# Casts and low parts of the mixer's weights at first rank in the scheduler's order

## The chip, the cores and the metric

The kernel runs on one core of a Trainium2 chip. The metric is the device time of one execution in microseconds. A core has engines that each take their own instructions one after the other and that wait for each other by semaphores: TensorE (PE in the profile, with its weight loads as PEld), VectorE (DVE), ScalarE (ACT), GpSimd (POOL) and SyncE (SP), which here only issues DMAs.

## The reference

One decoder layer on 256 tokens of width 2048 in float32: a feed-forward network, a token mixer, and a second feed-forward network, each with a residual sum and a layer norm behind it.

```python
x = layer_norm(ALPHA * x + 0.5 * swiglu(x, ffn1_w_gate, ffn1_w_up, ffn1_w_down), ln1_g, ln1_b)
(c_q, c_kv, k_rope, q_nsa, k_c, v_c, k_s, v_s, k_w, v_w, g_nsa) = split_cols(x @ w_in, IN_SIZES)
o_mla = mla_attention(c_q, c_kv, k_rope, ...)        # 8 heads, latent ranks 512 and 256, causal softmax
o_nsa = nsa_attention(q_nsa, k_c, v_c, k_s, ...)     # 8 heads: compressed, selected and window branch, gated
mix = jnp.concatenate([o_mla, o_nsa], axis=-1) @ w_out
x = layer_norm(ALPHA * x + mix, ln2_g, ln2_b)
x = layer_norm(ALPHA * x + 0.5 * swiglu(x, ffn2_w_gate, ffn2_w_up, ffn2_w_down), ln3_g, ln3_b)
```

The hidden width of the feed-forward networks is 5632. The mixer's weights are w_in (2048 columns in, 3416 out), two up-projections of the latent attention (uq and ukv), the small matrices of the block compression, and w_out (2048 x 2048).

## The kernel before

**Three products for one.** [...] `split(hi, lo, src)` (L94 to L96) does this: ACT casts the source to the high part (L95), and DVE subtracts the high part from the source, which gives the low part (L96). `mm3` (L98 to L102) then issues three matmuls into one PSUM bank: high by high (L100), high activations by low weights (L101), low activations by high weights (L102). In the names of the profile, `whi` and `wlo` are the parts of a weight piece, `thi` and `tlo` those of transposed activations; `raw` and `sum` are the buffers into which the pieces are loaded.

**Buffers.** A weight piece is 128 x 1024 values (two blocks of 128 rows, 512 columns). Raw pieces come into 5 buffers of the pool `rawp` or 3 of `sump`, by turns. The high parts have 6 buffers (`hip`), the low parts 6 (`lop`). So a cast needs three things: its piece has landed, one of the 6 high buffers has been released by TensorE's last matmul on it, and ACT is free. [...]

**The mixer's weights** all come through `load` (L149). It issues the DMA on SP (L171, or the paired form above it), takes a high and a low buffer, and splits. With `spare` set it splits into tiles of the attention's pool instead and returns earlier (L172 to L178); this is so for the first two pieces of the mixer's first product. `load` is called by `gemm` (input projection, ukv, output projection), `gemm_T` (the up-projections whose result is wanted transposed) and `out_last` (the last columns of w_out). The feed-forward weights do not come this way: `gemm2` splits them itself, in its inner function `parts`.

**Order of the work.** The order of PE and SP is that of the program text (`manual_schedule` for these two engines). The other engines are ordered by the scheduler of the Tile layer when the program is built: it keeps a timeline of its own, and where several instructions of one engine are ready, the one with the best rank goes first. The rank is the place in the program text, unless the instruction stands in a `tc.high_priority()` block, which gives it a rank at the start of the program. At run time each engine keeps the order that came out of this, and waits at an instruction whose inputs or buffers are not ready, with all that stands behind it.

In the kernel before, two things stand in such blocks: the normalisation of a row block in `ln` (from the mean and variance, L598, to the scaling of the rows, L610 and L612), and, with `first` set, the scaling and the split of the first transposed tile behind a layer norm in `norm_T` (L577 to L588).

**Attention beside the projections.** The text interleaves large products with small work by hand. A product counts time in ticks, `tick(n)` advances them, and generators that were given to `spawn` run on between the pieces: each yields a number of ticks and so sets how far behind an evaluation on ACT and DVE the dependent instruction of PE is placed. For a softmax this is DSM = 4 ticks; two ticks are one piece, 12 matmuls of 512 columns. A softmax unit runs through: scores from PSUM with scale and mask on DVE (L804), row maximum on DVE (L777), exponentials on ACT (L781), their sums and reciprocals on DVE (L788, L789, with a gate L791), scaling of the rows on ACT (L794) or DVE (L796), transposes on PE (L812), and the copy of these to SBUF on ACT (L814). The block compression has a chain of small steps on DVE and ACT (L969 to L975, a gelu), matmuls from raw buffers (L956) and a last matmul (L980 or L986). `ln_res` (L622 to L630) multiplies the residual rows by gain and bias on DVE; nothing waits for it before the output projection. `norm_T` transposes rows on PE (L575), scales them on ACT (L583, for even groups of four columns) or DVE (L585), and splits them (L95 and L96 with `thi` and `tlo`).

In the text, a weight piece's split stands directly ahead of its own matmuls. The softmax steps of an earlier tick stand ahead of it.

Of the kernel before, what the change touches and what calls it, by code (L numbers as in the profile page):

```python
# [53 lines left out]
def layer(ctx: ExitStack, tc: tile.TileContext, a: dict, out: bass.AP):  # L54
# [24 lines left out]
    def am2(dt=F32):  # L79

        m = am(dt)
        return m[:, 0:4, :], m[:, 4:8, :]
# [11 lines left out]
    def split(hi, lo, src):  # L94
        A.copy(hi, src)  # L95
        V.tensor_tensor(lo, src, f(hi), op=OP.subtract)  # L96
# [45 lines left out]
    def new_raw():  # L142

        turn[0] += 1
        return (sump if turn[0] % 8 >= 5 else rawp).tile([P, KT, NCH], F32, name="sum" if turn[0] % 8 >= 5 else "raw")
# [3 lines left out]
    def load(w, c, pc, spare=False):  # L149

        if (id(w), c, pc[0]) in ahead:
            return ahead.pop((id(w), c, pc[0]))
        ap, pairs, n = w[:3]
        paired = len(w) > 3
        k0, kn = pc[0], len(pc)
        assert pc == list(range(k0, k0 + kn)) and k0 // KT == pc[-1] // KT
        r0 = (c * pairs + k0 // KT) * P
        raw = new_raw()
        order = list(range(kn))
        if paired:  # L160

            r0 = (c // 2 * pairs + k0 // KT) * P
            src = w[3][r0:r0 + P].rearrange("p (i j n) -> p i j n", i=2, j=2)[:, :, c % 2, :]
            if c % 2:
                order = order[::-1]
            if kn < KT:
                at = k0 % KT if c % 2 == 0 else 1 - k0 % KT
                src = src[:, at:at + 1]
            nc.sync.dma_start(raw[:, :kn, :n], src)
        else:  # L170
            nc.sync.dma_start(raw[:, :kn, :n], ap[r0:r0 + P].rearrange("p (k n) -> p k n", k=KT)[:, k0 % KT:k0 % KT + kn])  # L171
        if spare:  # L172
            out = []
            for j in range(kn):
                hi, lo = (m.rearrange("p a b -> p (a b)")[:, :n] for m in am2(F32R))
                split(hi, lo, raw[:, j, :n])
                out.append((hi, lo))
            return [out[j] for j in order]  # L178
        hi = hip.tile([P, KT, NCH], F32R, name="whi")
        lo = lop.tile([P, KT, NCH], F32R, name="wlo")  # L180
        split(hi[:, :kn, :n], lo[:, :kn, :n], raw[:, :kn, :n])
        return [(hi[:, j, :n], lo[:, j, :n]) for j in order]

    def new_bank():
# [2 lines left out]
    def gemm(x, w, c, ks, finish, head=0, tail=0, spare=0, first=KT, each=None, nxt=None):  # L187
# [20 lines left out]
        for r in ([pcs[:head]] if head else []) + mid + ([pcs[len(pcs) - tail:]] if tail else []):  # L208
            end = r[-1] is pcs[-1]
            held = []  # L210
            for pc in r:
                held.append((pc, load(w, c, pc, at == 0 and len(held) < spare)))
                go(0, *held[-1])
                if len(r) > 1:
                    tick(1)
            if end:
                if nxt:
                    ahead[id(nxt[0]), nxt[1], nxt[2]] = load(nxt[0], nxt[1], [nxt[2] + j for j in range(KT)])
                finish(0, ps[0])
            for h in held:  # L220
                go(1, *h)
                if len(r) > 1:
                    tick(1)
            if end:
                finish(1, ps[1])
            if len(r) == 1:
                tick(2)
            if each:
                each(at)
            at += 1  # L230

    def gemm_T(xs, w, c, ks, finish, nxt):

        wp = {}
        for i in range(0, len(ks), KT):
            wp.update(zip(ks[i:i + KT], load(w, c, ks[i:i + KT])))
        nb = w[2] // P  # L240
        for i in range(nb // 2):
            ps = new_bank().rearrange("p (b s) -> p b s", b=2)
            for j in range(2):
                cs = slice((2 * i + j) * P, (2 * i + j + 1) * P)
                for k in ks:
                    (wh, wl), (xh, xl) = wp[k], xs(k)
                    PE.matmul(ps[:, j], wh[:, cs], xh, start=k == ks[0], stop=False)
                    PE.matmul(ps[:, j], wh[:, cs], xl, start=False, stop=False)
                    PE.matmul(ps[:, j], wl[:, cs], xh, start=False, stop=k == ks[-1])
                tick(1)  # L250
            if i == nb // 2 - 1 and nxt:
                ahead[id(nxt[0]), nxt[1], nxt[2]] = load(nxt[0], nxt[1], [nxt[2] + j for j in range(KT)])
            finish(i, ps)
# [942 lines left out]
```

## Time and profile before

| | us |
|---|---|
| three runs | 1755.46 (median), 1753.73, 1756.78 |
| the profiled execution | 1755.67 |
| its span, first to last instruction | 1754.0 |

The granted clock of TensorE was 0.998 over the span. By the windows of busy time, with the borders rounded to where the stages change, in us:

| stage | length | TensorE | VectorE | ScalarE |
|---|---|---|---|---|
| first feed-forward network, 0 to 690 | 690 | 685.87 | 656.76 | 418.67 |
| its end, the mixer, 690 to 1040 | 350 | 347.47 | 241.70 | 181.30 |
| second layer norm, second network, last layer norm, 1040 to 1754 | 714 | 702.02 | 688.37 | 421.82 |

How to read the rows that follow. A group has line, engine, operation, the tile that is written and those that are read, shapes and count; behind the first bar stand the busy time and the mean in ns of one, behind the second the idle time of the engine just before and what ended it. In the timeline a row has start, duration and the instruction; "x2" is two in a row merged into one, and the bracket names the idle time of that engine before it and what ended it. Ends of matmuls are modelled and overlap the next start, so for TensorE the distance from start to start is what counts. In the DMA rows the last number is the median time from issue to landing.

### The profile page before, as it was taken

Reading aid. Unit: us, or ns where it says so; the run is one execution under the profiler, and the core shown is the slowest. Engines: PE = TensorE matmul, PEld = TensorE weight load, DVE = VectorE, ACT = ScalarE, POOL = GpSimd, SP = SyncE. Lnnn points to the kernel's source line nnn. Section 1 sums busy time; section 2 is a strip of 40 time slices with the busy share of each in tenths; the row PEclk is TensorE's granted clock in tenths of the full one; section 3 lists DMA queues with packets and bytes.
Section 4 is the critical chain, followed back from the end, with each engine's and each line's share of the span. In section 5 each row is a group of like instructions: output and inputs, shape, how many; then the busy total and the mean of one; then the engine's idle time right before and its main releaser. Section 6 shows DMA issues by size and latency. Waiting matters only on the chain. (4 is left out here: it accounts for less than half of the span.)

```text
span 1754.0 us, 22419 instructions
## 1 busy us (share of the span) xinstructions
PE 1735.4 (99%) x8040; PEld 1428.0 (81%) x8040; DVE 1586.8 (90%) x2099; ACT 1021.8 (58%) x1354; POOL 17.0 (1%) x39
## 2 busy tenths in 40 slices
PE   9999999999999999999999999999999999999997
PEld 7888888887888888887788788888888888888886
DVE  7899999999999999865586679899999999999998
ACT  6656565565656656654365555565665565656652
POOL 0000000000000000000000001000000000000000
PEclk9999999999999999999999999999999999999999
DMA  9665656555666457646753355655666555565655
GB/s 334 220 214 167 213 197 214 192 192 190 210 204 229 172 196 245 192 156 214 260 193 120 122 179 170 214 192 172 212 206 211 202 192 199 197 211 193 205 202 181
DMA packets 100336, 350.01 MB, mean 200 GB/s; under 512 B 11136, under 2 KB 13696, under 8 KB 100224
## 3 DMA queue, kind: packets, MB, share of 16 engines
q1 hardware_dynamic: 98944, 344.39, 58.2%
q0 software_dynamic: 1280, 4.20, 0.9%
q8 instruction: 63, 1.03, 0.2%
q14 instruction: 49, 0.40, 0.1%
HBM read 346.44 MB, written 2.10 MB: 199 GB/s over the span
## 5 line engine op out<-in xcount | busy, mean ns | idle before, releaser
L100 PE MATMUL bank<-whi,thi 128*128 128x512 f32 (+1 forms) x1904 | 747.9, 393 | 0.6 <-ACT whi L95 0.6
L101 PE MATMUL bank<-wlo,thi 128*128 128x512 f32 (+1 forms) x1904 | 740.3, 389 | 3.1 <-DVE wlo L96 3.1
L102 PE MATMUL bank<-whi,tlo 128*128 128x512 f32 (+1 forms) x1904 | 739.5, 388 | 0.0
L95 ACT CAST whi<-raw 128x1024 fp32r<-128x1024 f32 (+1 forms) x577 | 539.9, 962 | 265.1 <-PE bank L102 140.1
L96 DVE TENSOR_TENSOR wlo<-raw,whi 128x1024 fp32r<-128x1024 f32 (+1 forms) x577 | 630.9, 1109 | 60.5 <-ACT whi L95 59.2
L95 ACT CAST whi<-sum 128x1024 fp32r<-128x1024 f32 x271 | 282.6, 1049 | 341.6 <-DVE sum L328 137.5
L100 PEld LDWEIGHTS bank<-whi,thi 128*128 128x128 f32 x1904 | 357.7, 188 | 78.1 <-issue 4.1
L101 PEld LDWEIGHTS bank<-wlo,thi 128*128 128x128 f32 x1904 | 357.8, 188 | 77.4 <-DVE wlo L96 6.5
L102 PEld LDWEIGHTS bank<-whi,tlo 128*128 128x128 f32 x1904 | 357.5, 188 | 73.5
L96 DVE TENSOR_TENSOR wlo<-sum,whi 128x1024 fp32r<-128x1024 f32 x271 | 324.7, 1216 | 30.9 <-ACT whi L95 28.9
L101 PE MATMUL bank<-wlo,m 128*128 128x512 f32 x448 | 174.4, 389 | 0.4 <-DVE wlo L96 0.4
L102 PE MATMUL bank<-whi,m 128*128 128x512 f32 x448 | 174.3, 389 | 0.0
L100 PE MATMUL bank<-whi,m 128*128 128x512 f32 x448 | 174.3, 389 | 0.0
L326 DVE TENSOR_TENSOR sum<-raw 128x1024 f32<-128x1024 f32 x112 | 136.6, 1220 | 11.2 <-DMA raw<-in_ffn_w_up 9.0
L101 PEld LDWEIGHTS bank<-wlo,m 128*128 128x128 f32 x448 | 84.1, 188 | 18.5 <-DVE wlo L96 0.9
L102 PEld LDWEIGHTS bank<-whi,m 128*128 128x128 f32 x448 | 84.1, 188 | 17.4
L100 PEld LDWEIGHTS bank<-whi,m 128*128 128x128 f32 x448 | 84.1, 188 | 17.4
L328 DVE TENSOR_TENSOR sum<-sum,raw 128x512 f32<-128x512 f32 x112 | 76.7, 685 | 0.2
L327 DVE TENSOR_TENSOR sum<-sum,raw 128x512 f32<-128x512 f32 x112 | 76.7, 685 | 0.1
L384 DVE TENSOR_TENSOR w<-bank,w 128x512 f32<-128x512 f32 x80 | 51.8, 682 | 1.4 <-PE bank L102 1.4
L781 ACT ACTIVATE w<-w,mx 128x256 f32<-128x256 f32 (+1 forms) x48 | 21.3, 446 | 27.7 <-DVE mx L777 24.7
L516 DVE TENSOR_TENSOR w<-w 128x512 f32<-128x512 f32 x40 | 25.7, 684 | 0.0
(187 smaller groups left out, 938.4 us busy)
## 6 DMA issues: line engine op xcount, KB each, us to landing
raw<-in_ffn_w_down SPq DMA_DIRECT2D x176, 512.0 KB, 4.4
raw<-in_ffn_w_up SPq DMA_DIRECT2D x160, 512.0 KB, 4.8
raw<-in_ffn_w_gate SPq DMA_DIRECT2D x146, 512.0 KB, 4.8
raw<-in_ffn_gu SPq DMA_DIRECT2D x32, 512.0 KB, 4.9
raw<-in_w_in SPq DMA_DIRECT2D x30, 512.0 KB, 5.3
raw<-in_w_out SPq DMA_DIRECT2D x20, 512.0 KB, 3.3
sum<-in_w_in SPq DMA_DIRECT2D x18, 512.0 KB, 5.5
sum<-in_ffn_w_gate SPq DMA_DIRECT2D x12, 512.0 KB, 4.8
```

Source lines behind the costliest of these rows:

```text
L95: A.copy(hi, src)
L96: V.tensor_tensor(lo, src, f(hi), op=OP.subtract)
L100: PE.matmul(ps, xh, wh, start=first and not onto, stop=False, skip_group_check=onto)
L101: PE.matmul(ps, xh, wl, start=False, stop=False, skip_group_check=onto)
L102: PE.matmul(ps, xl, wh, start=False, stop=last, skip_group_check=onto)
L326: V.tensor_tensor(t13, a_, b_[:, 1:2, :].broadcast_to([P, 2, NCH]), op=OP.add)
L327: V.tensor_tensor(t24[:, 0], t13[:, 0], a_[:, 1], op=OP.add)
L328: V.tensor_tensor(t24[:, 1], t24[:, 0], b_[:, 0], op=OP.add)
L384: V.tensor_tensor(r, B[b], rest[b], op=OP.add)
L516: V.tensor_tensor(hs[c0 + j, t], r, sg[c0 + j, t], op=OP.mult)
L781: A.activation(s[:, h, :], s[:, h, :], AF.Exp, bias=mx[:, h:h + 1], accum_out=sm[:, h:h + 1])
```

## The change

The call of `split` for pieces that go to the high and low buffers, in `load`, stands in a `tc.high_priority()` block. Casts and subtractions of the mixer's weights so get a rank at the start of the program; the two spare pieces, the feed-forward weights, and the splits of activations keep theirs. The DMA stays outside the block.

```diff
@@ -178,7 +178,8 @@
             return [out[j] for j in order]
         hi = hip.tile([P, KT, NCH], F32R, name="whi")
         lo = lop.tile([P, KT, NCH], F32R, name="wlo")
-        split(hi[:, :kn, :n], lo[:, :kn, :n], raw[:, :kn, :n])
+        with tc.high_priority():
+            split(hi[:, :kn, :n], lo[:, :kn, :n], raw[:, :kn, :n])
         return [(hi[:, j, :n], lo[:, j, :n]) for j in order]
```

## The prediction

> **What bounds the kernel now.** I read the page's engine shares first, then busy time by window, the groups of the mixer (690 to 1040 us), its waits, and the timeline around each wait.
>
> ```profile
> span 1754.0 us, 22419 instructions
> PE 1735.4 (99%) x8040; PEld 1428.0 (81%) x8040; DVE 1586.8 (90%) x2099; ACT 1021.8 (58%) x1354; POOL 17.0 (1%) x39
> ```
>
> TensorE is busy 99% of the span. The profiled execution took 1755.67 us, 1.67 more than its span and 0.2 above the median of 1755.46, so sums against it need no correction that matters.
>
> ```profile
> 690.00:1040.00 350.00, 347.47 (x1846) 283.10 (x1845) 241.70 (x443) 181.30 (x348) 8.33 (x14) 1.00 0.55 185
> 1100.00:1150.00 50.00, 50.00 (x222) 41.41 (x221) 47.53 (x53) 27.17 (x30) 0.00 (x0) 1.00 0.57 192
> ```
>
> Columns: the window, its length, then busy time and count for PE, PEld, DVE, ACT and POOL, the granted clock, DMA share and GB/s. The first row holds the mixer, which the change touches; the second is a feed-forward stretch without a gap. The mixer leaves TensorE idle for 2.53 us. Busy time hides more, because matmuls overlap: 222 in 50 us is one per 225 ns, while the rows below give each some 390 ns. A wait must therefore be read from starts. VectorE (69%) and ScalarE (52%) have room there.
>
> ```profile
> PE bank L101 <- DVE wlo L96: 0.9, 1, 0.9
> PE bank L100 <- ACT whi L95: 0.5, 1, 0.5
> PE bank L812 <- DVE w L796: 0.4, 1, 0.4
> PE bank L102 <- DVE tlo L96: 0.3, 1, 0.3
> PE bank L100 <- ACT thi L95: 0.2, 1, 0.2
> ```
>
> These are all waits of TensorE in the mixer: total, times, longest. Only the first two are for a weight's high or low part, one event each, and both belong to one place, near 873 us. The others wait for normalised rows or a softmax. So what the change can give is worth one stall, and what it can cost is spread over everything that it overtakes.
>
> **The change part by part.** It adds and removes no instruction, DMA or buffer. PE and SP run in the written order. What moves are the casts (ACT) and subtractions (DVE) of the mixer's weights.
>
> ```profile
> L95 ACT CAST whi<-raw 128x1024 fp32r<-128x1024 f32 (+1 forms) x60 | 61.1, 1026 | 56.7 <-PE bank L102 31.3 <-DMA raw<-in_mla_w_ukv 11.3 <-issue 7.7
> L95 ACT CAST whi<-sum 128x1024 fp32r<-128x1024 f32 (+1 forms) x36 | 36.6, 1024 | 30.0 <-PE bank L102 20.9 <-DMA sum<-in_w_in 7.9 <-ACT thi L95 0.7
> L96 DVE TENSOR_TENSOR wlo<-raw,whi 128x1024 fp32r<-128x1024 f32 (+1 forms) x60 | 71.1, 1191 | 37.0 <-ACT whi L95 36.9
> L96 DVE TENSOR_TENSOR wlo<-sum,whi 128x1024 fp32r<-128x1024 f32 (+1 forms) x36 | 42.6, 1188 | 22.2 <-ACT whi L95 22.1
> ```
>
> That is 96 pairs, each 1.03 us on ACT and 1.19 on DVE. Most cannot move: ACT already idled 52.2 us (31.3 + 20.9) directly before such casts, waiting for TensorE to free a buffer. A cast that starts when its buffer comes free gains nothing from rank. Rank counts only where a ready cast or subtraction and something else compete. There the weight now goes first and the other work comes later by one cast (1.03) or one subtraction (1.19), or by several. I price four such places.
>
> *The stall at 873, a possible gain.*
>
> ```profile
> 867.26 0.59 PE L871 MATMUL bank<-krT,m 128*128 128x256 f32 x2
> 867.51 0.58 PE L100 MATMUL bank<-whi,thi 128*128 128x512 f32 x1
> 867.93 0.39 PE L101 MATMUL bank<-wlo,thi 128*128 128x512 f32 x1
> 871.74 0.59 PE L871 MATMUL bank<-krT,m 128*128 128x256 f32 x2
> 872.83 0.51 PE L100 MATMUL bank<-whi,thi 128*128 128x512 f32 x1 [0.49 <-ACT whi L95]
> 874.25 0.50 PE L101 MATMUL bank<-wlo,thi 128*128 128x512 f32 x1 [0.92 <-DVE wlo L96]
> ...
> 869.34 0.51 ACT L781 ACTIVATE w<-w,mx 128x256 f32<-128x256 f32 x1 [2.97 <-DVE mx L777]
> 870.93 0.91 ACT L794 ACTIVATE w<-w,rs 128x256 f32<-128x256 f32 x2 [0.49 <-DVE rs L789]
> 871.74 1.98 ACT L95 CAST whi<-sum 128x1024 fp32r<-128x1024 f32 x2
> ...
> 857.90 1.27 SPq L171 DMA_DIRECT2D sum<-in_w_in  x2
> ...
> sum<-in_w_in SPq DMA_DIRECT2D x3, 512.0 KB, 9.1
> ```
>
> In the earlier group L100 follows L871 by 0.25 and L101 by 0.67, so at the second L101 was due at 872.41; it came at 874.25, 1.84 late. The cast it needs stood on ACT behind a softmax (L781, L794). The loads were issued by 859.17 and landed about 9.1 us later, near 868, while ACT stood idle for 2.97 us before L781. This speaks against a gain: an idle ACT takes whatever is ready, of whatever rank, so when the order was made the casts were not ready (the order assumes later landings than the chip's), and rank does not alter that. I take 0; the ends are 0 and -1.84.
>
> *First layer norm.*
>
> ```profile
> 700.82 1.05 ACT L95 CAST whi<-sum 128x1024 fp32r<-128x1024 f32 x1
> 701.75 0.63 ACT L95 CAST thi<-w 128x512 fp32r<-128x512 f32 x1
> 702.27 1.06 ACT L95 CAST whi<-sum 128x1024 fp32r<-128x1024 f32 x1
> ...
> 702.43 0.50 PE L100 MATMUL bank<-m,thi 128*128 128x512 f32 x1 [0.21 <-ACT thi L95]
> ```
>
> TensorE starts 0.05 after thi ends (702.38). The next weight cast follows thi without idle time, so it may have been ready; ahead of thi it costs 0.93 (700.82 to 701.75, one cast from start to start), less the slack 0.05: +0.9. The low part on DVE can be pushed by a subtraction too: ends 0 and +2.1 (0.9 and one 1.19).
>
> *Softmax before 891.*
>
> ```profile
> 886.07 2.35 DVE L96 TENSOR_TENSOR wlo<-raw,whi 128x1024 fp32r<-128x1024 f32 x2
> 890.54 0.68 DVE L796 TENSOR_TENSOR w<-w,rs 128x512 f32<-128x512 f32 x1
> 891.37 0.63 PE L812 MATMUL bank<-ident,w 128*128 128x128 f32 x4 [0.40 <-DVE w L796]
> ```
>
> TensorE's transpose starts 0.15 after L796. Two subtractions stand behind the earlier steps of this softmax; put before them they shift the chain by one to two subtractions, less what they no longer take later. One, less the slack 0.15, is +1.0; ends 0 and +2.2 (2.35 less 0.15).
>
> *Sparse attention near 917.*
>
> ```profile
> 914.57 0.49 ACT L781 ACTIVATE w<-w,mx 128x256 f32<-128x256 f32 x1
> 915.55 1.03 ACT L95 CAST whi<-sum 128x1024 fp32r<-128x1024 f32 x1
> 916.57 0.91 ACT L794 ACTIVATE w<-w,rs 128x256 f32<-128x256 f32 x2
> 916.78 1.30 PE L812 MATMUL bank<-ident,w 128*128 128x128 f32 x8
> ```
>
> The transposes begin before L794 ends (917.48), so half of them have no slack. The cast at 915.55 follows two exponentials without idle time. Ahead of them it delays L794 by 1.03, less about 0.1: +0.95; ends 0 and +2.0, if the next cast also overtakes L794.
>
> The other softmaxes lose up to a cast, too, but I found them with more room; for those that are as tight I keep +1 for the range only. Earlier subtractions free raw buffers sooner, so SP's loads can start sooner; since TensorE waits for weights at one place, that is worth nothing beyond the 1.84.
>
> The sum: 1755.67 + 0 + 0.9 + 1.0 + 0.95 = **1758.5 us**, +0.17% over the median.
>
> [...] In the rows above weight loads fill 80.9% of the mixer (283.10 of 350) and 82.8% of the gapless stretch (41.41 of 50). [...]
>
> **The rivals.**
> - *Slower, a blocked ACT.* A cast with first rank is put ahead of a ready softmax step though its buffer is not free yet; the engine then stands.
>
> ```profile
> 886.40 1.05 ACT L95 CAST whi<-sum 128x1024 fp32r<-128x1024 f32 x1 [2.17 <-PE bank L102]
> 887.35 0.25 ACT L973 ACTIVATE gu<-gu 128x64 f32<-128x64 f32 x1
> ...
> ACT whi L95 <- PE bank L102: 52.2, 41, 2.3
> ```
>
> Here ACT stood 2.17 us for TensorE. The mean such wait in the mixer is 52.2/41 = 1.27. With the cast that is 2.3 us at a tight softmax; about four tight ones give +9, with the layer norm +10: 1765. It decides from the second softmax without slack. For it: 52.2 us of such waits. Against: they hardly reach TensorE today. [...]
> - *Nothing counts.* Readiness sets the order nearly everywhere, and what swaps has slack: 1755.5. For it: the idle 52.2 us.
> - *Faster.* The stall at 873 goes and no new one comes: 1755.67 - 1.84 = 1753.8. [...]
>
> **How the numbers follow.** A measurement of this kernel can tell about 0.2% (3.5 us) from no change. Chances: the forecast case (some tight chains lose a cast or a subtraction, up to +7.3, the sum of the terms' ends and the extra 1) 0.62; nothing counts 0.17; faster by the one stall 0.08; faster by hidden time 0.04; blocked ACT 0.09. The range, 1753 to 1764, takes in the stall's removal and all ends of the forecast case (1755.67 + 7.3 = 1763.0); hidden time and blocked ACT lie outside, 0.13 together. Of the forecast case I put 0.30 under +3.5 and 0.32 over it: its value taken is +2.85, but its ends reach further up. So faster 0.04 (hidden time alone); same 0.30 + 0.17 + 0.08 = 0.55; slower 0.32 + 0.09 = 0.41. The direction is fairly sure, the size is small.
>
> **What would show it.** Right: the feed-forward parts unchanged; matmul count equal; near 702, 891 and 917 TensorE waits for thi, L796 and L794 longer than now; ACT shows casts before those steps. The gain of 0 at 873 is wrong if the casts start before L781 there. Blocked ACT shows as more idle time before casts released by PE with a softmax step behind them. I am wrong altogether if the mixer ends earlier by over 2 us, or if TensorE waits for weights at a place where it does not today.

## The result and the profile after

| | before | after |
|---|---|---|
| median of four runs, us | 1755.36 (1753.73 to 1756.78) | 1764.97 (1763.84 to 1766.00) |
| ratio, 95% interval | | 1.0059 (1.0047 to 1.0071) |
| profiled execution, us | 1755.67 | 1764.27 |
| its span, us | 1754.0 | 1762.5 |

The change makes the kernel 9.6 us slower. That is 0.97 us above the upper end of the range, and on the side that had 0.41. From L181 on, lines of the changed kernel are one higher than before.

The head of its page has the engines' busy times:

```profile
PE 1736.5 (99%) x8040; PEld 1428.9 (81%) x8040; DVE 1588.4 (90%) x2099; ACT 1024.6 (58%) x1354; POOL 16.4 (1%) x39
```

The counts of the five engines' work are those of before and TensorE is busy 1.1 us more, so the time is not more work but waiting, and a lower clock behind one of the waits. The table of busy time by window (columns as before: length, then PE, PEld, DVE, ACT, POOL, clock, DMA share, GB/s) says where:

```profile
690.00:1048.50 358.50, 347.91 (x1837) 282.25 (x1836) 240.58 (x440) 181.45 (x347) 7.77 (x14) 1.00 0.52 178
1048.50:1762.50 714.00, 702.01 (x3152) 580.67 (x3150) 689.02 (x858) 422.78 (x504) 6.92 (x12) 1.00 0.59 196
```

The second part is 714 us long as before (714, TensorE busy 702.02 then). The mixer went from 350 us with 347.47 us of TensorE to 358.50 with 347.91: the idle time rose from 2.5 to 10.6 us. TensorE's waits in it (total, times, longest):

```profile
PE bank L100 <- ACT thi L95: 3.2, 1, 3.2
PE bank L813 <- ACT w L795: 1.9, 2, 1.2
PE bank L879 <- ACT w L815: 1.6, 1, 1.6
PE bank L813 <- DVE w L797: 1.2, 1, 1.2
PE bank L101 <- DVE wlo L96: 0.9, 1, 0.9
PE bank L813 <- DVE pc L786: 0.6, 1, 0.6
PE bank L1007 <- DVE pc L797: 0.6, 1, 0.6
PE bank L100 <- ACT whi L95: 0.5, 1, 0.5
```

The two waits for a weight, 0.9 and 0.5, are what they were. All the new ones are for what the weights overtook: a layer norm tile (`thi`), scaled probabilities (`w` of L795 and L797, `pc`) and a copy of turned probabilities (`w` of L815).

To give each place its price I set every matmul's start against that of the same matmul before. Both traces hold 8040 in the same order, so the growth of the difference between two marks is the time lost there. Marks are times of the kernel before.

| mark to mark, us | lost, us | what TensorE waits for |
|---|---|---|
| 692 to 716 | 4.24 | first tile of the layer norm, then a lower clock |
| 716 to 884 | 0.02 | (holds the stall at 873) |
| 884 to 892 | 2.69 | copy L815 (1.78, and 0.1 right behind it), scaled rows L797 (0.8) |
| 892 to 930 | 1.34 | scaled rows L795 near 917 |
| 930 to 975 | 1.39 | `pc` near 957 and 965 |
| 975 to 1040 | 1.02 | scaled rows L795 near 996 |
| sum | 10.70 | |

From 1040 to the end it is -0.1. In the first network, whose program text is the same, this execution gained 2.0 us on that of before; 10.7 less 2.0 and 0.1 is the 8.6 us by which the last matmuls are late.

**The first layer norm.** The timeline of ScalarE and then TensorE, changed kernel:

```profile
695.52 1.05 ACT L95 CAST whi<-raw 128x1024 fp32r<-128x1024 f32 x1 [0.44 <-ACT y L613]
696.48 2.00 ACT L95 CAST whi<-sum 128x1024 fp32r<-128x1024 f32 x2
698.38 0.45 ACT L584 ACTIVATE w<-bank,pack 128x128 f32<-128x128 f32 x1
698.73 1.04 ACT L95 CAST whi<-sum 128x1024 fp32r<-128x1024 f32 x1
699.67 1.98 ACT L95 CAST whi<-raw 128x1024 fp32r<-128x1024 f32 x2
701.56 1.15 ACT L584 ACTIVATE w<-bank,pack 128x128 f32<-128x128 f32 x3
702.74 0.62 ACT L95 CAST thi<-w 128x512 fp32r<-128x512 f32 x1
...
703.41 0.50 PE L100 MATMUL bank<-m,thi 128*128 128x512 f32 x1 [3.19 <-ACT thi L95]
```

Before, one cast stood between the four scalings (L583, 699.44) and `thi`. Now three stand between the first scaling and the other three. Then TensorE's clock falls. The windows after that wait, changed kernel (the third-last number of a row is the granted clock):

```profile
702.00:704.00 2.00, 0.59 (x2) 0.30 (x2) 2.00 (x3) 1.97 (x7) 0.00 (x0) 1.00 1.00 296
704.00:706.00 2.00, 1.98 (x8) 1.42 (x8) 1.99 (x6) 1.34 (x5) 0.00 (x0) 0.72 1.01 334
706.00:708.00 2.00, 2.00 (x7) 1.66 (x6) 1.42 (x3) 0.56 (x2) 0.00 (x0) 0.50 0.29 105
708.00:710.00 2.00, 2.00 (x9) 1.62 (x8) 1.91 (x7) 0.05 (x1) 0.33 (x1) 0.93 0.00 0
```

Of the 4.24 us, 2.98 are lost before the first matmul of the product and 1.26 behind it.

**A blocked copy near 888.** Changed kernel, ScalarE and then TensorE:

```profile
888.65 1.04 ACT L95 CAST whi<-sum 128x1024 fp32r<-128x1024 f32 x1 [2.71 <-PE bank L102]
889.60 0.58 ACT L815 COPY w<-bank 128x512 f32<-128x512 f32 x1
...
890.23 1.16 PE L879 MATMUL bank<-w,m 128*128 128x128 f32 x8 [1.62 <-ACT w L815]
```

Kernel before, the same two instructions of ScalarE in the other order (its cast with the wait of 2.17 us is in the prediction):

```profile
883.64 0.59 ACT L814 COPY w<-bank 128x512 f32<-128x512 f32 x1
```

**The softmax near 917**, changed kernel, ScalarE and then TensorE:

```profile
919.49 1.03 ACT L95 CAST whi<-sum 128x1024 fp32r<-128x1024 f32 x1
...
920.93 0.49 ACT L782 ACTIVATE w<-w,mx 128x256 f32<-128x256 f32 x1
...
921.94 1.04 ACT L95 CAST whi<-sum 128x1024 fp32r<-128x1024 f32 x1 [0.42 <-ACT w L782]
922.89 0.90 ACT L795 ACTIVATE w<-w,rs 128x256 f32<-128x256 f32 x2
...
923.45 0.95 PE L813 MATMUL bank<-ident,w 128*128 128x128 f32 x4 [1.15 <-ACT w L795]
```

Before, one cast stood between the last exponential and the scaling (915.55, in the prediction). Now that one stands ahead of the last two exponentials, and a second has come in between them and the scaling that TensorE waits for.

### The profile page after: what moved, and what is told of

Its sections match the earlier page's. It is cut to its first block, busy times and chain, and to the rows that moved or that the text cites. A ratio compares the mean times of both kernels' runs of the same rounds, so it can differ in the third digit from the quotient of the medians.

```text
span 1762.5 us, 22438 instructions
## 1 busy us (share of the span) xinstructions
PE 1736.5 (99%) x8040; PEld 1428.9 (81%) x8040; DVE 1588.4 (90%) x2099; ACT 1024.6 (58%) x1354; POOL 16.4 (1%) x39
## 3 DMA queue, kind: packets, MB, share of 16 engines
q8 instruction: 63, 1.03, 0.2%
## 5 line engine op out<-in xcount | busy, mean ns | idle before, releaser
L385 DVE TENSOR_TENSOR w<-bank,w 128x512 f32<-128x512 f32 x80 | 52.0, 688 | 1.6 <-PE bank L102 1.6
```

Source lines behind the costliest of these rows:

```text
L385: V.tensor_tensor(r, B[b], rest[b], op=OP.add)
```

## The experiments

In the table are the times against runs of the kernel before on the same chip, and the time lost between marks in each profiled execution, as above. "716 to 884" is left out: it is 0.04 or less in all but one run, which is told of there. The first network, ahead of 692, is left out too: there the executions differ from that of before by -2.7 to +1.4 us, and all_first by +3.1 (two waits of 0.6 and 0.8 us for weights near 689; its granted clock was 0.995 over the span, 0.998 before). A row therefore need not add up to its median.

| run | over before, us | ratio, 95% interval | 692-716 | 884-892 | 892-1040 | 1040-end |
|---|---|---|---|---|---|---|
| changed kernel, again | 10.5 | 1.0058 (1.0045 to 1.0070) | 4.96 | 2.69 | 3.77 | 1.34 |
| first_only | 4.6 | 1.0026 (1.0016 to 1.0035) | 4.18 | 0.00 | 0.00 | -0.26 |
| middle_only | 2.0 | 1.0010 (1.0001 to 1.0019) | -0.01 | 1.62 | -0.03 | -0.26 |
| late_only | 8.0 | 1.0041 (1.0028 to 1.0054) | -0.02 | 3.06 | 4.94 | -0.21 |
| warm | 9.9 | 1.0057 (1.0044 to 1.0071) | 3.16 | 2.69 | 3.74 | 0.18 |
| cast_only | 8.6 | 1.0047 (1.0034 to 1.0060) | 4.33 | -0.44 | 3.58 | 1.52 |
| sub_only | 9.7 | 1.0052 (1.0038 to 1.0066) | 4.50 | 3.45 | 0.08 | 0.32 |
| rank100 | 11.1 | 1.0063 (1.0050 to 1.0076) | 3.22 | 2.69 | 3.76 | 0.63 |
| tiles_first | 17.6 | 1.0094 (1.0080 to 1.0108) | 6.04 | 2.69 | 3.78 | 3.56 |
| all_first | 11.6 | 1.0064 (1.0052 to 1.0077) | 6.30 | -0.45 | 1.00 | 3.74 |
| users_first | 4.2 | 1.0021 (1.0012 to 1.0030) | -0.07 | -0.44 | 0.85 | 5.41 |
| chain_first | 10.8 | 1.0060 (1.0048 to 1.0073) | 6.17 | -0.43 | 1.02 | 0.89 |
| ordered | 4.2 | 1.0023 (1.0014 to 1.0032) | 0.57 | -0.44 | 1.03 | 1.33 |

Between 692 and 1040 the steps repeat from one execution to the next to 0.04 us, except where a lower clock is in them. That makes them the better instrument for a single place; the medians say whether they add up. Behind 1040 they don't repeat: two executions of the changed kernel gave -0.1 and 1.34 there, so differences of that size in the last column say nothing.

The theory after the result: the loss is a sum of places at which a chain that TensorE soon needs was overtaken. The rivals: ScalarE blocked by casts without a buffer, everywhere; the low parts on VectorE; two engines over-full at the first product, so that no order helps.

### The rank for a part of the loads

```diff
-        with tc.high_priority():
+        with tc.high_priority() if stage[0] == 0 else nullcontext():   # first_only; 1: middle_only, 2: late_only
```

`stage[0]` becomes 1 behind the call for the first product and 2 ahead of `nsa_att(0)`.

> The first rank is given to the casts and low parts of the first product's weights alone (those loaded ahead of the first layer norm's end). Theory 'a sum of places' (each place at which the order changed keeps its own price): the first product's start is late by the 4.3 us of the changed kernel, of which about 1.3 us by a lower granted clock after the idle gap; the middle and the sparse attention stay as before: about 1759.7 us, +4.3. Rival 'blocked ACT' (casts that wait for TensorE to free their weight buffer hold up the copies behind them): the first product's casts find free buffers, so about 1755.5, no change. Rival 'one common cause in the number of early instructions' (20 of 67 moved ACT instructions): about +2.9, 1758.3.

> The first rank is given to the weights loaded between the first product and the first block of the sparse attention. Theory 'a sum of places': the wait of the cast at 888 us for its buffer (1.8 us), the softmax near 891 (0.8), nothing else: about 1758.0 us, +2.6, with TensorE idle some 1.6 us for the copy behind that cast. Rival 'blocked ACT everywhere': the casts with the longest waits (59 and 41 us) lie here too, so most of the whole loss, +6 or more, 1761.5 or above. If the stall at 888 isn't there while the rest of the order is as in the changed kernel, it hung on a shift from the first product: about +0.8, 1756.3.

> The first rank is given to the weights loaded from the first block of the sparse attention on. Theory 'a sum of places': the softmaxes near 917 (1.3 us), 957 (0.7), 965 (0.7) and 997 (0.95) are late by the casts that come in between their exponentials or ahead of the copy of the probabilities: about 1759.0 us, +3.5; TensorE's waits for the copies of L795 appear, the first product and the stretch to 896 us are as before. Rival 'what is late at 917 and after is only what was pushed there from 703 and 888': within 0.5 us of before, 1755.5. Rival 'blocked ACT': a cast with a wait for a weight buffer of over 1 us stands ahead of each loss.

first_only came to +4.6 where +4.3 was foretold, and middle_only to +2.0 where +2.6 was; each has its loss at its own place and none elsewhere. In middle_only the copy is late as foretold, but the softmax near 891 isn't, so 1.62 us are lost there and not 2.6. late_only came to +8.0 instead of +3.5. The softmaxes cost what was foretold (1.43, 1.39 and 1.04 at the same three places), and a new wait near 890 makes up the rest. VectorE, TensorE and a window of late_only:

```profile
885.91 2.35 DVE L96 TENSOR_TENSOR wlo<-sum,whi 128x1024 fp32r<-128x1024 f32 x2
...
888.73 1.23 DVE L96 TENSOR_TENSOR wlo<-sum,whi 128x1024 fp32r<-128x1024 f32 x1 [0.28 <-ACT whi L95]
889.87 0.22 DVE L977 TENSOR_TENSOR hid<-gu,gx 128x64 f32<-128x64 f32 x1
...
890.19 1.03 PE L988 MATMUL bank<-w,hid 128*16 128x128 f32 x8 [2.62 <-issue]
...
892.00:894.00 2.00, 2.00 (x8) 1.61 (x7) 1.81 (x4) 0.59 (x1) 0.00 (x0) 0.50 0.96 387
```

Three more low parts than before stand ahead of the last step of the compression's gelu (`hid`, L977), for which TensorE waits 2.62 us; the profile puts that wait down to "issue", but the matmul starts 0.1 us after `hid` ends. The granted clock behind it was 0.50 in the window above and 0.74 in the next (894 to 896), and 892 to 912 is 1.08 us longer. So the three parts add to 14.6 us where the whole costs 9.6 to 10.5: a place's price depends on what stands in front, and prices found apart don't add. The rival "pushed there from 703 and 888" falls with late_only. "Blocked ScalarE everywhere" falls for the middle with middle_only; its expectation misread a row, in which 59 is a total and 41 a count. The casts' waits for a buffer in middle_only between 716 and 912 us (total, times, longest) are

```profile
ACT whi L95 <- PE bank L102: 24.0, 19, 2.7
```

and only one of these 19 reaches TensorE, near 885.

### Matmuls in the first wait

```diff
                 held.append((pc, load(w, c, pc, at == 0 and len(held) < spare)))
+                if head and len(held) == 1:
+                    hi0, lo0 = held[0][1][0]
+                    for _ in range(12):
+                        PE.matmul(ps[0], lo0[:, :P], hi0, start=True, stop=True)
```

> The changed kernel with twelve extra matmuls on the first weight's pieces, into a bank that the first product's first real matmul overwrites, so that TensorE is busy in the gap before the first layer norm's end. If the lower granted clock behind that gap (0.72, 0.50, 0.93 in the three 2-us windows after it) comes from the idle time: the clock stays near 1.00 there and the run is about 1.3 us faster than the changed kernel, 1763.6 us. If the lower clock was an accident of the one profiled execution: equal to the changed kernel, 1765.0. If the extra matmuls end after the real input is ready: up to 1 us slower, 1766.

The windows of warm that answer to those above:

```profile
704.00:706.00 2.00, 2.00 (x12) 1.64 (x12) 2.00 (x6) 1.24 (x3) 0.00 (x0) 1.00 0.89 295
706.00:708.00 2.00, 2.00 (x11) 1.63 (x10) 2.00 (x6) 0.00 (x0) 0.00 (x0) 1.00 0.01 5
```

The clock stays at 1.00. The first product starts 2.99 us late, as in the changed kernel (2.98), and 0.17 us are lost behind that instead of 1.26: the idle time causes the lower clock, and 1.1 us of the loss is by the clock (1.8 against the second execution of the changed kernel, with a clock of 0.60, 0.50, 0.50 and 0.70 in the windows from 702 to 710 us). In the medians this cannot be seen: the intervals of warm and of the changed kernel overlap almost wholly.

### The cast alone, the low part alone, and the kernel again

```diff
 # cast_only; sub_only has the block around the second line instead
-        split(hi[:, :kn, :n], lo[:, :kn, :n], raw[:, :kn, :n])
+            A.copy(hi[:, :kn, :n], raw[:, :kn, :n])
+        V.tensor_tensor(lo[:, :kn, :n], raw[:, :kn, :n], f(hi[:, :kn, :n]), op=OP.subtract)
```

> The changed kernel itself, beside the kernel before on this chip, so that the variants can be held against it. If the drifts of TensorE's starts in the mixer (10.6 us in all) carry the loss: 9 to 11 us over before, with the same places as before: 3.2 us of waiting ahead of the first product, 1.6 at the copy near 890, 1.9 at the two softmaxes of the sparse attention.

> Only ScalarE's cast of each weight has the first rank; the low part on VectorE keeps the old one. Theory 'casts overtake or block what stands on ScalarE': the first product (4.3 us), the copy near 890 (1.8), the softmaxes near 917 (1.3) and 997 (0.95) are as in the changed kernel, +8 us over before. Rival 'the low parts do it' (eight first pieces' subtractions ahead of the layer norm's on VectorE): the first product starts as before or within 1 us, and the whole loss is under 4 us.

> Only VectorE's subtraction has the first rank; the casts keep the old one. Theory 'casts overtake or block': only the waits that the profile of the changed kernel puts on VectorE are left (near 891, 957 and 965: 0.8 + 0.7 + 0.7), +2.2 us over before, and the first product's wait is below 1.5 us. Rival 'the low parts do it': the first product's wait of about 3 us is there, +6 us or more.

The changed kernel repeats. cast_only met its +8, with one miss: the copy near 890 is not late. sub_only missed by far: +9.7 for the +2.2 foretold. Its wait ahead of the first product is gone, but 4.5 us are lost in the same stretch for the second row tile. And it has the blocked copy, with all casts at the old rank. ScalarE in sub_only:

```profile
891.99 1.04 ACT L181 CAST whi<-sum 128x1024 fp32r<-128x1024 f32 x1 [2.72 <-PE bank L102]
892.94 0.58 ACT L816 COPY w<-bank 128x512 f32<-128x512 f32 x1
```

So that block doesn't need a cast of first rank. Why the two stand in this order there, no run shows. Sparse attention splits cleanly: 3.58 with the casts, 0.08 with the low parts. The first product does not: either alone costs the whole 4.2 to 4.5. Neither rival had that.

### The weights behind the layer norm's first tile

In ScalarE's rows above three casts stand between the first scaling and the other three, although the scalings are in a first-rank block, too. rank100 gives the weights' pair a rank behind that block.

```diff
-        with tc.high_priority():
+        with tc.high_priority(offset=tc.cur_priority - 100):
```

> The changed kernel, but the weights' two instructions are given rank 100 and 101 rather than 0 and 1. [...] Theory: the first product's wait falls back from 3.2 to below 1 us and the granted clock stays near 1.00: 4.3 us less than the changed kernel, about +5.5 over before. Rival (VectorE and ScalarE are simply too late for the tile, whoever goes first, since weights that were put in the queues before it is ready cannot be overtaken any more): within 1 us of the changed kernel.

ScalarE runs the four scalings without a cast in between again (x4 from 698.20 us), and the wait of 3.2 us is gone, but the time did not fall: 3.22 us are lost a little later. TensorE's waits in that stretch are below. The first row holds two, 1.4 and the 0.2 that was there before; of the last row 0.3 was there before:

```profile
PE bank L100 <- ACT thi L95: 1.6, 2, 1.4
PE bank L576 <- DVE y L611: 0.7, 1, 0.7
PE bank L102 <- DVE tlo L96: 0.6, 1, 0.6
```

VectorE in rank100:

```profile
703.54 2.35 DVE L96 TENSOR_TENSOR wlo<-raw,whi 128x1024 fp32r<-128x1024 f32 x2
...
706.14 0.68 DVE L385 TENSOR_TENSOR y<-bank,w 128x512 f32<-128x512 f32 x1
...
710.48 1.00 DVE L611 TENSOR_SCALAR y<-y,mv,rstd 128x512 f32<-128x512 f32 x2
```

The kernel before had the first and the last of that chain here:

```profile
702.17 0.68 DVE L384 TENSOR_TENSOR y<-bank,w 128x512 f32<-128x512 f32 x1
...
706.70 1.00 DVE L610 TENSOR_SCALAR y<-y,mv,rstd 128x512 f32<-128x512 f32 x2
```

The last eviction of the first network (L385) now stands behind the low parts, so the second row tile is normalised 3.8 us later; TensorE's 0.7 for `y` is for it. The 1.4 is for a later tile of the first row tile, whose scaling on VectorE (L586) stands behind the same low parts. The rival was right about the time, but not yet shown to be right about the reason.

### What TensorE waits for, first

tiles_first adds the first rank for all tiles of the layer norm to rank100; all_first adds it for softmaxes, copies and the compression's gelu; users_first has both on the kernel before, the weights at their old rank.

```diff
-        with tc.high_priority() if first else nullcontext():
+        with tc.high_priority():                                  # norm_T, scalings; likewise its splits
...
+        with tc.high_priority():                                  # causal; likewise cmp, compress and the copies
             softmax(sv, K, None, gate, nh)
```

> As the run with rank 100 for the weights, and in addition every layer norm tile's evictions and splits (eight tiles, not the first alone) are put first, ahead of the weights. Theory 'the first product's stretch is short of ScalarE and VectorE, and it counts whether the norm's tiles or the weights go first': the 3.2 us that the run with rank 100 still lost between 692 and 716 us (in later waits, for the second tiles) fall below 1 us; the rest of the mixer loses its 6.4 us as before, so about +6.5 over before. Rival 'the two engines are simply over-full there': the loss stays at 3 us or more, +9.

> As the run with all tiles first, and the softmaxes, the copies of the turned probabilities and the small chain of the compression are put first too, ahead of the weights, which keep rank 100. Theory 'every loss is a consumer overtaken': the steps near 890 (2.7 us) and between 892 and 1040 us (3.75 us) go too, apart from what a blocked cast costs (a cast that waits for TensorE's release of its buffer holds the copy behind it, whatever the copy's rank, if the cast came to ScalarE before the copy was ready: up to 1.8 us near 886 to 890). So between +0 and +2.5 over before. Rival 'blocked and over-full engines, rank doesn't matter': +6 or more.

> The kernel before, with the weights at their old rank, and the layer norm tiles, the softmaxes, the copies of the turned probabilities and the compression's chain put first: the opposite of the change. Theory: TensorE's waits that are left in the mixer of the kernel before (0.6 + 0.5 us ahead of the first product, 0.4 near 891, 1.95 near 873) are in part for these users; up to 1.5 us faster than before, about -1. Rival 'what is late then are the weights': TensorE waits for a cast or a low part instead, 1 us slower or more.

all_first confirms the middle and the late part: -0.45 and 1.00 us instead of 2.69 and 3.75, the same to 0.15 us as users_first, where the weights have no rank. The copy near 890 is no longer behind a waiting cast, though the expectation allowed it to stay. ScalarE in all_first:

```profile
892.05 1.05 ACT L95 CAST whi<-sum 128x1024 fp32r<-128x1024 f32 x1
893.06 0.59 ACT L818 COPY w<-bank 128x512 f32<-128x512 f32 x1
```

The first product got worse, not better: 6.0 and 6.3 us. The wait of tiles_first there:

```profile
PE bank L576 <- DVE y L612: 4.0, 1, 4.0
```

Tiles and weights now alternate ahead of the second row tile's eviction, which has neither rank (it comes at 708.57, against 702.17 before). The tiles alone don't do that: users_first loses nothing there (-0.07). It was to be 1 us faster and is 4.2 slower, by 5.41 us behind 1040. Of that, 3.8 us are at the second layer norm, by the same kind of wait, and tiles_first and all_first lose the same 3.8 there, so it goes with the tiles' rank:

```profile
1056.95 0.55 PE L575 MATMUL bank<-ident,y 128*128 128x128 f32 x3 [2.78 <-DVE y L611]
```

The other 1.6 are within what executions differ by behind 1040.

### The second row tile's chain first

chain_first: all_first with the old rank for the tiles other than the first, and the eviction (L385) and the statistics (L566) first. ordered: the same with the tiles at rank 20, between that chain and the weights.

```diff
+                with tc.high_priority():
                     V.tensor_tensor(r, B[b], rest[b], op=OP.add)
...
+        with tc.high_priority():
             V.bn_stats(st[t][:, n, :], y[t][:, n * NCH:(n + 1) * NCH])
...
+        with tc.high_priority(offset=tc.cur_priority - 20):       # ordered only, norm_T
```

> Weights at rank 100; softmaxes, copies of the turned probabilities and compression first as before; and in addition the last eviction of the first feed-forward's second row tile and its layer norm statistics are put first, so that no weight's low part stands ahead of the second row tile's chain on VectorE. The layer norm's other tiles keep the old rank, behind the weights. Theory 'the second row tile's chain is what TensorE waits for in the end of that stretch' (in the run with rank 100 its eviction was at 706.14 us behind six low parts): the step between 692 and 716 us falls from 3.2 us to about 1. Rival 'the tiles' evictions behind the weights carry it': 2.5 us or more. Between 884 and 1040 us the +0.6 net of the run with all users first.

> As the run before, but the layer norm's tiles get rank 20: eviction, statistics and normalization first, then the tiles, then the weights at rank 100. The weights still go ahead of all the work with an ordinary rank (ropes, copies of queries and keys, residuals). Theory 'every loss is one overtaken chain': the step between 692 and 716 us is within 0.5 us of zero, that between 884 and 1040 us about +0.6 net; the second layer norm (1040 to 1400 us) may lose or gain by the same ranks. Time by the mixer alone: 1754 + 1 us. Rival 'over-full engines': 3 us or more between 692 and 716.

chain_first was to fall to about 1 us and lost 6.17 there, for the next tile in turn:

```profile
710.38 0.80 PE L100 MATMUL bank<-whi,thi 128*128 128x512 f32 x1 [4.76 <-ACT thi L95]
```

ordered loses 0.57. So the engines are not over-full; whichever link of the chain stands behind the weights is the one that TensorE waits for, and only when eviction, statistics, normalisation and tiles are all ahead does the loss go. chain_first is also the one run with a loss between 716 and 884, 1.91 us: behind the stall near 873 the granted clock was 0.71 and 0.50 in the two windows from 880 us.

ordered is 4.2 us slower than before, so no version here beats it. Its mixer from 692 to 1040 loses 1.2 us; the rest of the 4.2 lies outside, where the eviction's new rank also acts in the first network (1.3 us near 222; 1.0 in chain_first, which has that rank too), and was not taken apart further.

## Why the prediction failed, step by step

**What bounds the kernel: right.** TensorE stayed busy 99% of the span, and the change cost waits, and a lower clock behind one of them, in the mixer only, spread over what the weights overtake.

**The stall at 873, taken at 0: right.** The reason given, that the casts were not ready when the order was made, was an estimate; it fits every run: the stall stands in all of them, and in all but chain_first with these sizes. Changed kernel:

```profile
875.08 0.50 PE L100 MATMUL bank<-whi,thi 128*128 128x512 f32 x1 [0.48 <-ACT whi L95]
876.51 0.50 PE L101 MATMUL bank<-wlo,thi 128*128 128x512 f32 x1 [0.93 <-DVE wlo L96]
```

Against 0.49 and 0.92 before.

**First layer norm, +0.9 with an end of +2.1: the step that failed.** It measured 4.24 and, again, 4.96. The working looked at the one cast behind `thi` and put it ahead. It priced nothing ahead of the four scalings, which stand in a first-rank block themselves, and stopped at the first matmul. Three things were left out. The scalings are overtaken as well (three casts came in between 698.73 and 701.56). Put the tile first again (rank100), and 3.2 us are still lost, because the next links are overtaken: the later tiles' scalings on VectorE, and the second row tile's eviction. And the idle time costs clock, 0.50 to 0.93 in the windows behind it: 1.1 to 1.8 us more (warm). The term should have been worked out for the whole chain of both row tiles, in a stretch that was full: the window of the kernel before from 698 to 712 us has VectorE busy 13.27 and ScalarE 13.73 of 14 us, which the mixer's means of 69% and 52% hid:

```profile
698.00:712.00 14.00, 13.46 (x70) 10.74 (x69) 13.27 (x25) 13.73 (x25) 0.56 (x1) 1.00 0.31 89
```

**Softmax before 891, +1.0: right in mechanism and about right in size**, 0.8. It is the low parts, as the working had it: with the casts alone at first rank this stretch gains 0.44, with the low parts alone it loses 3.45, of which the copy is 1.9. But in the changed kernel, too, 1.78 us were lost just ahead of it for the blocked copy. The forecast had the row of that very cast with its wait of 2.17 us, in the rival, and didn't ask what stood on ScalarE just in front of it (the copy at 883.64) and could come behind.

**Sparse attention near 917, +0.95: near in size, 1.32, but by another way, so in part by luck.** The cast at 915.55 stood ahead of the scaling L794 already. Put ahead of the two exponentials it leaves ScalarE as much to do before L794 as it had. It no longer fills the wait for the reciprocals behind the last exponential, and that can cost some 0.5 us (an estimate from the 0.49 ahead of L794 at 870.93). The rest came of the next cast (921.94), which the prediction had only as an end of the range, and which itself stood blocked for 0.42 us.

**"I found them with more room": wrong.** The softmaxes near 957, 965 and 996 lost 0.72, 0.74 and 0.95, each somewhat less than one cast (1.03). They had next to no room, and the prediction shows no row for them. Casts alone make nearly all of it (3.58 of 3.75 in cast_only).

**The rivals.** "A blocked ACT" gave 1765, the time that came, but not for its reason. It wanted four waits of 2.3 us; there is one place, near 888, worth 1.78, and a block of 0.42 near 917. Many casts still wait for a buffer (19 between 716 and 912 us in middle_only), and nearly all of these waits end without TensorE noticing. Its chance of 0.09 was for the mechanism; the time was carried by the first layer norm and by three softmaxes thought safe. "Nothing counts" and both kinds of "faster" fell: the changed kernel gains at none of these places. (cast_only gains 0.44 near 891, where the wait of 0.40 for the softmax goes.) No run shows a hidden time, on which a chance of 0.04 was put; in the mixer TensorE's busy time went from 347.47 to 347.91 us, its idle time from 2.5 to 10.6.

**The sum** was 2.85 where 10.7 came: 3.3 to 4.1 short at the first layer norm, 1.8 at the copy, 2.4 at the later softmaxes, 0.2 at 891 and 917 together. The range ended 1 us above the terms' ends and the 1 us kept for the other softmaxes. It had hardly any room for a place that wasn't on the list.

## What to carry to other kernels

Giving producers a better rank helps only where the consumer waits for them; elsewhere a chain with less slack than one instruction can lose, and the whole chain must be followed, evictions and statistics included, since the loss moves to the first link left behind. Price such a change in the window where the engines are full, not by a stage's mean, and leave room in the range for places not found. Prices of parts do not add, so the whole must be measured.

## What was not expected of the hardware

A wait of TensorE can cost more than itself. With matmuls in the gap of the first product (warm) the granted clock stayed at 1.00; behind the 3.19 us there it fell, and so it did behind these other waits (windows of 2 us, from the first below 1.00):

| run | wait, us | window from, us | granted clock |
|---|---|---|---|
| changed kernel | 3.19 | 704 | 0.72, 0.50, 0.93 |
| changed kernel, again | 3.2 | 702 | 0.60, 0.50, 0.50, 0.70 |
| first_only | 3.2 | 702 | 0.77, 0.50, 0.87 |
| cast_only | 3.4 | 704 | 0.89, 0.50, 0.76 |
| tiles_first | 4.0 | 710 | 0.83, 0.50, 0.82 |
| chain_first | 4.76 | 710 | 0.54, 0.61 |
| late_only | 2.62 | 890 | 0.90, 0.50, 0.74 |
| users_first | 2.78 | 1057 | 0.68, 0.50, 0.96 |

In the changed kernel the clock was 0.50 from 704.87 to 708.28 us, for 3.41 us, and 1.00 on both sides. The length is not the same each time: the same wait of 3.2 us cost 1.26 us behind it in one execution of the changed kernel and 1.97 in the other.

After the stall near 873, whose two gaps of 0.5 and 0.9 us stand in all these runs (0.8 and 0.8 in chain_first), it fell in chain_first; the others lose 0.04 us or less between 716 and 884:

```profile
882.00:884.00 2.00, 2.00 (x6) 1.59 (x5) 1.40 (x3) 1.58 (x3) 0.00 (x0) 0.50 0.83 244
```

The wait of 1.62 us near 890 in the changed kernel left the clock at 1.00 (888 to 900 us), and rank100, with waits of 1.4, 0.7 and 0.6 us behind the layer norm, had 0.998 over the span, as before. So a fall came behind two gaps of 0.8 us near each other and none behind one of 1.62; what decides that, these runs don't show.
